# The moving operands of the projections are shifted by 16 bytes against the weights

## The chip, the cores and the metric

The kernel is one program on one core of a Trainium2 chip. The metric is the device time of one execution in microseconds (us): 2906.49 us is the median of three runs of the kernel before (2905.98 to 2910.71).

## The reference

Two blocks of two layers each work on x, 512 tokens by 1024 features in float32. Every layer has a mixer (mLSTM with neighbourhood attention, differential attention, HGRN2 with forgetting attention, RG-LRU with stick-breaking attention) and a gated feed-forward; the first block also has cross attention to 256 memory tokens. Each sublayer ends in a projection, a residual sum and a layer norm. What matters here are the products with the weight matrices:

```
proj = x @ w_in                       # mixers, q/k/v, memory
mix  = heads @ w_out
gate, up = split(x @ w_gu)            # 1024 -> 2 * 2816
ff   = (silu(gate) * up) @ w_down     # 2816 -> 1024
x    = layer_norm(alpha * x + mix or ff)
```

## The kernel before

x lies transposed, features on the 128 partitions, in eight tiles of 512 tokens. Every product is made of two float32r parts per operand: a high part (the rounded number) and a low part (the remainder). `mm3` (L271 to L276) issues three matmuls for each pair of 128 x 128 weights and 128 x 512 x: high with high (L274), weights high with x low (L275), weights low with x high (L276). In its call `matmul(out, a, b)` the first operand a is loaded into the array as weights (LDWEIGHTS, the stationary operand) and b streams past it (the moving operand). So each of the three has a weight load of its own, and TensorE alternates weight load, matmul, weight load, matmul. The program lists the matmuls' operands as moving,stationary: `p_mm<-xh,w_hi` is x's high part moving past the high part of the weights, into the PSUM tile `p_mm`.

`fetch` (L326) brings 128 x 1024 weights by DMA into `w_raw`, ScalarE rounds them into `w_hi` (L337), VectorE takes the remainder into `w_lo` (L339). `block_a` (L342) runs eight k-steps of `mm3` over one such block, 24 matmuls. `proj_a` (L349) does so for a list of blocks, either over all 512 tokens or, with `halves`, over 256 tokens at a time; `close_sublayer` (L411) always works on 256 tokens at a time. `proj_b` (L378) turns the roles round: parts of x (or of the memory) are the stationary operand and the weights move.

The operands of these products are: `XH` and `XL` (x's parts, tiles `xh`, `xl`, L219 and L220), the inner features of the feed-forward (`f_h`, `f_l`, L556 and L557), the parts of the memory (`mm_h`, `mm_l`, L603), keys, queries and values of the attentions, and `w_hi`, `w_lo`. A tile is a range of bytes in every partition of SBUF, laid down by the pools in the order of the program. No engine's order of work is touched here; the order is that of the code.

Where the tiles start, in bytes of a partition, modulo 256:

```
                      before                      after the change
w_hi, w_lo (all)      32                          32
xh, xl (x's parts)    32                          48
f_h, f_l              32                          48
mm_h, mm_l, m_kh      224                         224
x_qh, x_ql            32                          32
x_ph, x_pl            96                          96
m_v                   224                         224
dv / d_pt             128 / 0                     128 / 0
```

A slice of 128 or 256 float32 columns moves the start by a multiple of 256 bytes, so these remainders hold for every matmul on the tile.

Of the kernel before, what the change touches and what calls it, by code (L numbers as in the profile page):

```python
# [9 lines left out]
F32R = mybir.dt.float32r  # L10
# [6 lines left out]
P = 128  # L17
S = 512
D = 1024
KT = 8  # L20
# [33 lines left out]
def layout(i):  # L54
# [62 lines left out]
    for l in range(2):  # L117
        ffn(f"f{l}", f["ffn_w_gu"][l], f["ffn_w_down"][l])
        ffn(f"f{l + 2}", f["ffn_w13_2"][l], f["ffn_w2_2"][l])
# [87 lines left out]
class Prog:  # L207
    def __init__(self, ctx, tc, a):
        self.tc, self.nc, self.a = tc, tc.nc, a
        nc = tc.nc  # L210
        self.cp = ctx.enter_context(tc.tile_pool(name="cst", bufs=1))
        self.st = ctx.enter_context(tc.tile_pool(name="state", bufs=1))
        self.wp = ctx.enter_context(tc.tile_pool(name="wts", bufs=4))
        self.ps = ctx.enter_context(tc.tile_pool(name="ps", bufs=4, space=PSUM))
        st = self.st
        xf = st.tile([P, KT * S], F32, name="xf")
        self.XF = [xf[:, k * S : (k + 1) * S] for k in range(KT)]
        self.all_x = xf.rearrange("p (k s) -> p k s", k=KT)
        self.XH = [st.tile([P, S], F32R, name=f"xh{k}") for k in range(KT)]  # L219
        self.XL = [st.tile([P, S], F32R, name=f"xl{k}") for k in range(KT)]  # L220
        self.AO = [st.tile([P, S], F32, name=f"ao{k}") for k in range(KT)]
        cp = self.cp

        ones = cp.tile([P, 2 * P], F32, name="k_ones")
        nc.vector.memset(ones[:, 0:P], 1.0 / D)
        nc.vector.memset(ones[:, P : 2 * P], 1.0 / P)
        self.ones_d, self.ones_p = ones[:, 0:P], ones[:, P : 2 * P]
        nr = cp.tile([P, P], F32R, name="k_nr")
        nc.vector.tensor_scalar(nr, ones[:, P : 2 * P], -float(P), None, ALU.mult)
        self.mones_r = nr  # L230
        pr = cp.tile([P, P], F32R, name="k_pr")
        nc.vector.tensor_copy(pr, ones[:, P : 2 * P])
        self.ones_pr = pr
        cc = cp.tile([P, 4], F32, name="k_cc")
        nc.vector.memset(cc[:, 0:1], LN_EPS)
        nc.vector.memset(cc[:, 1:2], 1.0)
        self.eps, self.one = cc[:, 0:1], cc[:, 1:2]
        self.kv = {}
        self.pending = []
        self.biases = []  # L240
        self.before = []
        self.loaded = False
# [306 lines left out]
    def ffn(self, pre, ln, last=False):  # L549
        nc, tc, a = self.nc, self.tc, self.a  # L550
        with tc.tile_pool(name="ffn", bufs=2, reuse_waits="tile") as fp:
            off = 0
            for part, nt in enumerate(FPARTS):
                hs, ls = [], []
                for t in range(nt):
                    hs.append(fp.tile([P, S], F32R, name="f_h", tag="f_h", bufs=11))  # L556
                    ls.append(fp.tile([P, S], F32R, name="f_l", tag="f_l", bufs=11))  # L557

                def evac(n, ps, c0, c1, keep={}):
                    t = n // 2  # L560
                    c = slice(c0, c1)
                    if n % 2 == 0:
                        s = fp.tile([P, S], F32, name="f_s", tag="f_s", bufs=3)
                        nc.scalar.activation(s[:, c], ps[:, c], AF.Silu)
                        keep[t, c0] = s
                    else:
                        s = keep.pop((t, c0))
                        nc.vector.tensor_tensor(s[:, c], s[:, c], ps[:, c], ALU.mult)  # L568
                        self.tail = self.split(hs[t][:, c], ls[t][:, c], s[:, c])

                src = []
                for t in range(nt):
                    src += [a[pre + "_gu"][off + t], a[pre + "_gu"][FT + off + t]]
                if part == 0:
                    self.proj_a(src[:4], evac, halves=True)
                    self.proj_a(src[4:], lambda n, ps, c0, c1: evac(n + 4, ps, c0, c1), tags=("mm", "sc"))
                else:
                    self.proj_a(src, evac, tags=("mm", "sc"))
                off += nt
                d = a[f"{pre}_d{part}"]  # L580
                if part < len(FPARTS) - 1:
                    for m in range(8):
                        w = self.fetch(d[m], nt * P)
                        ps = self.mm(("mm", "sc")[m % 2])
                        self.block_a(w, ps, hs, ls)
                        self.add_partial(m, ps, part == 0)
                else:
                    self.close_sublayer([d[m] for m in range(8)], hs, ls, False, ln, last)
# [1013 lines left out]
```

## Time and profile before

| | us |
|---|---|
| median of three runs | 2906.49 |
| the profiled execution | 2910.26 |
| span of its instructions | 2908.3 |
| TensorE matmul busy | 2849.4 (98% of the span) |
| VectorE busy | 1694.3 (58%) |
| ScalarE busy | 1274.8 (44%) |
| mean granted TensorE clock | 0.996 of 2.4 GHz |

[...] What a stream costs is read from one start to the next. [...]

### The profile page before, as it was taken

Reading aid. Unit: us, or ns where it says so; the run is one execution under the profiler, and the core shown is the slowest. Engines: PE = TensorE matmul, PEld = TensorE weight load, DVE = VectorE, ACT = ScalarE, POOL = GpSimd, SP = SyncE. Lnnn points to the kernel's source line nnn. Section 1 sums busy time; section 2 is a strip of 40 time slices with the busy share of each in tenths; the row PEclk is TensorE's granted clock in tenths of the full one; section 3 lists DMA queues with packets and bytes.
Section 4 is the critical chain, followed back from the end, with each engine's and each line's share of the span. In section 5 each row is a group of like instructions: output and inputs, shape, how many; then the busy total and the mean of one; then the engine's idle time right before and its main releaser. Section 6 shows DMA issues by size and latency. Waiting matters only on the chain.

```text
span 2908.3 us, 40029 instructions
## 1 busy us (share of the span) xinstructions
PE 2849.4 (98%) x15354; PEld 2415.0 (83%) x15354; DVE 1694.3 (58%) x3164; ACT 1274.8 (44%) x2328; POOL 424.1 (15%) x500
## 2 busy tenths in 40 slices
PE   9999999999999999999999999999999999999998
PEld 7678989888886678898888988798888976988887
DVE  5877656333469887563333767873333759733335
ACT  4555544222256765442222644652222548532223
POOL 0402012000121121020000432230000302400003
PEclk9999999999999999999999999999999999999999
DMA  5232522333332225223332321223332331133232
GB/s 179 78 117 77 160 66 88 95 98 98 101 97 80 76 70 170 71 80 101 93 99 79 106 73 60 80 88 95 100 96 83 99 93 39 59 103 100 94 94 67
DMA packets 83071, 269.07 MB, mean 93 GB/s; under 512 B 10648, under 2 KB 15144, under 8 KB 82880
## 3 DMA queue, kind: packets, MB, share of 16 engines
q1 hardware_dynamic: 81376, 261.49, 29.3%
q0 software_dynamic: 1504, 5.04, 0.5%
q8 instruction: 120, 1.97, 0.3%
q14 instruction: 71, 0.58, 0.1%
HBM read 260.14 MB, written 2.15 MB: 90 GB/s over the span
## 4 chain that ended last, share of the span: by engine, by line
PE 78%; DVE 13%; ACT 4%; issue 3%; DMA 1%; POOL 0%; SPq 0%; DVEq 0%; ACTq 0%; POOLq 0%
PE p_mm L275 14%; PE p_mm L274 13%; PE p_mm L276 13%; PE p_sc L274 10%; PE p_sc L276 10%; PE p_sc L275 9%; DVE w_lo L339 2%; DVE ao L450 2%; PE p_tp L275 1%; PE p_tp L276 1%; PE p_tp L274 1%; DVE ac L742 1%; DVE xl L460 1%; PE p_sc L1264 1%; DVE ao L449 1%
## 5 line engine op out<-in xcount | busy, mean ns | idle before, releaser
L337 ACT ACTIVATE w_hi<-w_raw 128x1024 fp32r<-128x1024 f32 (+2 forms) x478 | 492.9, 1036 | 1108.6 <-PE p_mm L275 484.1
L339 DVE TENSOR_TENSOR w_lo<-w_raw,w_hi 128x512 fp32r<-128x512 f32 (+2 forms) x956 | 650.1, 710 | 501.9 <-ACT w_hi L337 495.6
L274 PE MATMUL p_mm<-xh,w_hi 128*128 128x512 f32 (+1 forms) x1920 | 688.8, 359 | 7.3 <-ACT w_hi L337 4.9
L275 PE MATMUL p_mm<-xl,w_hi 128*128 128x512 f32 (+1 forms) x1920 | 688.1, 358 | 5.6 <-DVE xl L460 3.6
L276 PE MATMUL p_mm<-xh,w_lo 128*128 128x512 f32 (+1 forms) x1920 | 683.5, 356 | 0.0
L275 PEld LDWEIGHTS p_mm<-xl,w_hi 128*128 128x128 f32 x1920 | 365.2, 190 | 59.0 <-DVE xl L460 6.5
L274 PEld LDWEIGHTS p_mm<-xh,w_hi 128*128 128x128 f32 x1920 | 365.0, 190 | 58.7 <-ACT w_hi L337 4.9
L276 PEld LDWEIGHTS p_mm<-xh,w_lo 128*128 128x128 f32 x1920 | 365.0, 190 | 49.5 <-issue 0.6
L276 PE MATMUL p_sc<-xh,w_lo 128*128 128x512 f32 (+1 forms) x1024 | 358.5, 350 | 0.9 <-DVE w_lo L339 0.9
L274 PE MATMUL p_sc<-xh,w_hi 128*128 128x512 f32 (+1 forms) x1024 | 359.3, 351 | 0.0
L275 PE MATMUL p_sc<-xl,w_hi 128*128 128x512 f32 (+1 forms) x1024 | 358.0, 350 | 0.0
L496 POOL TENSOR_TENSOR ao<-xf 128x256 f32<-128x256 f32 x20 | 19.9, 995 | 1695.6 <-DVE xf L489 1293.8
L568 DVE TENSOR_TENSOR f_s<-f_s,p_sc 128x512 f32<-128x512 f32 x80 | 55.1, 688 | 289.4 <-PE p_sc L276 289.4
L276 PEld LDWEIGHTS p_sc<-xh,w_lo 128*128 128x128 f32 x1024 | 193.7, 189 | 26.4 <-DVE w_lo L339 1.1
L274 PEld LDWEIGHTS p_sc<-xh,w_hi 128*128 128x128 f32 x1024 | 193.6, 189 | 25.8 <-issue 0.4
L275 PEld LDWEIGHTS p_sc<-xl,w_hi 128*128 128x128 f32 x1024 | 193.7, 189 | 25.3 <-issue 0.2
L274 PE MATMUL p_sc<-f_h,w_hi 128*128 128x512 f32 (+1 forms) x464 | 157.5, 339 | 0.0
L276 PE MATMUL p_sc<-f_h,w_lo 128*128 128x512 f32 (+1 forms) x464 | 157.2, 339 | 0.2
L275 PE MATMUL p_mm<-f_l,w_hi 128*128 128x512 f32 (+1 forms) x464 | 157.2, 339 | 0.0
L276 PE MATMUL p_mm<-f_h,w_lo 128*128 128x512 f32 (+1 forms) x464 | 156.7, 338 | 0.0
L274 PE MATMUL p_mm<-f_h,w_hi 128*128 128x512 f32 (+1 forms) x464 | 156.7, 338 | 0.0
L275 PE MATMUL p_sc<-f_l,w_hi 128*128 128x512 f32 (+1 forms) x464 | 156.7, 338 | 0.0
(438 smaller groups left out, 4699.2 us busy)
## 6 DMA issues: line engine op xcount, KB each, us to landing
w_raw<-in_f_gu SPq DMA_DIRECT2D x176, 512.0 KB, 3.5
w_raw<-in_w_e SPq DMA_DIRECT2D x70, 512.0 KB, 3.6
w_raw<-in_w_x SPq DMA_DIRECT2D x64, 512.0 KB, 3.9
w_raw<-in_w_o SPq DMA_DIRECT2D x64, 512.0 KB, 3.7
w_raw<-in_f_d SPq DMA_DIRECT2D x64, 448.0 KB, 3.2
w_raw<-in_f_d SPq DMA_DIRECT2D x32, 512.0 KB, 3.5
r_s<-r_t SPq DMA_DIRECT2D x64, 64.0 KB, 2.0
na_b<-in_na_bias SPq DMA_DIRECT2D x6, 384.0 KB, 3.0
```

The lines of the kernel that those rows point to most:

```text
L274: nc.tensor.matmul(out, wh, xh, start=start, stop=False)
L275: nc.tensor.matmul(out, wh, xl, start=False, stop=False)
L276: self.last = nc.tensor.matmul(out, wl, xh, start=False, stop=stop)
L337: nc.scalar.activation(hi[:, :n], raw[:, :n], AF.Copy)
L339: nc.vector.tensor_tensor(lo[:, c], raw[:, c], hi[:, c].bitcast(F32), ALU.subtract)
L449: eng.tensor_tensor(t, self.XF[m][:, c], mu, ALU.subtract)
L450: nc.vector.scalar_tensor_tensor(t, t, g, r, ALU.mult, ALU.mult)
L460: nc.vector.scalar_tensor_tensor(xl, t, b, xh.bitcast(F32), ALU.add, ALU.subtract)
L496: eng.tensor_tensor(sm, self.XF[order[0]][:, c], self.XF[m][:, c], ALU.add)
L568: nc.vector.tensor_tensor(s[:, c], s[:, c], ps[:, c], ALU.mult)
L742: nc.vector.scalar_tensor_tensor(out, xp[:, j : j + S], w[j], out, ALU.mult, ALU.add)
L1264: nc.tensor.matmul(ps[:, c * 64 : c * 64 + 64].rearrange("p (n h) -> p n h", h=hl), x[:, cs], halves(x[:, cs], hl)[1], start=True, stop=True,)
```

## The change

All parts of x become slices of one tile `xs` that is 64 elements longer than its sixteen parts and skips its first 4 elements (16 bytes). Every tile of the inner features is made 64 elements (256 bytes) longer, and its first 4 elements are skipped. The weights' tiles start where they did, modulo 256. The engines issue the same instructions in the same order as before, with other addresses; one wait of ScalarE and four of the DMA queue name another matmul, since tiles that share room with them lie elsewhere.

```
-        self.XH = [st.tile([P, S], F32R, name=f"xh{k}") for k in range(KT)]
-        self.XL = [st.tile([P, S], F32R, name=f"xl{k}") for k in range(KT)]
+
+        xs = st.tile([P, 2 * KT * S + 64], F32R, name="xs")
+        xs = [xs[:, 4 + k * S : 4 + (k + 1) * S] for k in range(2 * KT)]
+        self.XH, self.XL = xs[:KT], xs[KT:]
...
-                    hs.append(fp.tile([P, S], F32R, name="f_h", tag="f_h", bufs=11))
-                    ls.append(fp.tile([P, S], F32R, name="f_l", tag="f_l", bufs=11))
+                    hs.append(fp.tile([P, S + 64], F32R, name="f_h", tag="f_h", bufs=11)[:, 4 : S + 4])
+                    ls.append(fp.tile([P, S + 64], F32R, name="f_l", tag="f_l", bufs=11)[:, 4 : S + 4])
```

## Rows read from the trace of the kernel before

**Rows 1.** The page: busy time of each engine, and the granted clock in 40 slices.

```profile
PE 2849.4 (98%) x15354; PEld 2415.0 (83%) x15354; DVE 1694.3 (58%) x3164; ACT 1274.8 (44%) x2328; POOL 424.1 (15%) x500
PEclk9999999999999999999999999999999999999999
```

**Rows 2.** TensorE's waits, longest in total first: us, times, longest.

```profile
PE p_mm L274 <- ACT w_hi L337: 4.9, 1, 4.9
PE p_sc L435 <- DVE ao L499: 4.4, 3, 1.8
PE p_mm L275 <- DVE xl L460: 3.6, 7, 0.9
```

**Rows 3.** Matmul groups by form: line, names, shape, count, busy us, mean ns.

```profile
L275 PE MATMUL p_mm<-xl,w_hi 128*128 128x512 f32 x1280 | 502.0, 392 | 0.0
L275 PE MATMUL p_sc<-xl,w_hi 128*128 128x512 f32 x640 | 249.0, 389 | 0.0
L275 PE MATMUL p_mm<-xl,w_hi 128*128 128x256 f32 x640 | 186.1, 291 | 5.6 <-DVE xl L460 3.6 <-POOL xl L463 1.7
L275 PE MATMUL p_sc<-xl,w_hi 128*128 128x256 f32 x384 | 109.0, 284 | 0.0
L275 PE MATMUL p_mm<-f_l,w_hi 128*128 128x512 f32 x240 | 93.4, 389 | 0.0
L275 PE MATMUL p_mm<-f_l,w_hi 128*128 128x256 f32 x224 | 63.8, 285 | 0.0
L275 PE MATMUL p_tp<-xl,w_hi 128*128 128x256 f32 x192 | 54.3, 283 | 0.0
L275 PE MATMUL p_mm<-w_lo,xh 128*128 128x512 f32 x96 | 37.4, 389 | 0.0
L276 PE MATMUL p_sc<-x_ph,m_v 128*128 128x512 f32 x32 | 12.6, 393 | 0.0
```

**Rows 4.** Timeline of TensorE, feed-forward, 512 tokens: start us, record's us.

```profile
1499.78 0.39 PE L274 MATMUL p_mm<-f_h,w_hi 128*128 128x512 f32 x1
...
1512.47 0.39 PE L276 MATMUL p_sc<-f_h,w_lo 128*128 128x512 f32 x1
```

**Rows 5.** The same, close of a feed-forward, 256 tokens.

```profile
799.80 0.28 PE L275 MATMUL p_sc<-f_l,w_hi 128*128 128x256 f32 x1
...
801.48 0.28 PE L274 MATMUL p_mm<-f_h,w_hi 128*128 128x256 f32 x1
```

**Rows 6.** The same, keys of the memory, 256 tokens.

```profile
309.77 0.28 PE L274 MATMUL p_mm<-mm_h,w_hi 128*128 128x256 f32 x1
...
312.61 0.28 PE L275 MATMUL p_sc<-mm_l,w_hi 128*128 128x256 f32 x1
```

**Rows 7.** Weight loads by form, in the stretch 800 to 812 us.

```profile
L274 PEld LDWEIGHTS p_mm<-f_h,w_hi 128*128 128x128 f32 x17 | 3.3, 192 | 0.0
```

**Rows 8.** Weight loads by form, in the stretch 306 to 312.9 us.

```profile
L274 PEld LDWEIGHTS p_mm<-mm_h,w_hi 128*128 128x128 f32 x8 | 1.5, 188 | 0.0
```

**Rows 9.** Weight loads by form, in the stretch 1500 to 1600 us.

```profile
L274 PEld LDWEIGHTS p_mm<-xh,w_hi 128*128 128x128 f32 x56 | 10.5, 188 | 2.2
```

**Rows 10.** Timeline of TensorE, values of the memory: weights move, memory parts stationary.

```profile
317.18 0.39 PE L275 MATMUL p_mm<-w_lo,mm_h 128*128 128x512 f32 x1
...
320.84 0.39 PE L276 MATMUL p_mm<-w_hi,mm_l 128*128 128x512 f32 x1
```

**Rows 11.** Timeline and group of the float32 values product in differential attention.

```profile
934.59 3.59 PE L1152 MATMUL p_tp<-d_pt,dv 128*128 128x512 f32 x8
L1152 PE MATMUL p_tp<-d_pt,dv 128*128 128x512 f32 x56 | 25.4, 596 | 0.4 <-DVE d_pt L1147 0.3
```

**Rows 12.** Stretches: busy us (and instructions) of PE, PEld, DVE, ACT, POOL; clock, DMA.

```profile
491.00:790.00 299.00, 298.96 (x1357) 249.01 (x1356) 109.12 (x172) 80.44 (x99) 3.19 (x4) 1.00 0.30 94
790.10:813.30 23.20, 23.20 (x193) 23.10 (x192) 17.51 (x34) 11.39 (x23) 11.26 (x13) 1.00 0.37 112
814.00:831.80 17.80, 17.80 (x109) 15.76 (x108) 16.34 (x37) 11.49 (x25) 8.99 (x11) 1.00 0.34 105
```

**Rows 13.** ScalarE groups of 128 x 512 that write from PSUM.

```profile
L816 ACT ACTIVATE xp<-p_mm 128x512 f32<-128x512 f32 x8 | 4.6, 580 | 0.0
L264 ACT ACTIVATE x_qh<-p_mm 128x512 fp32r<-128x512 f32 x16 | 9.3, 581 | 0.0
```

## The prediction

> **What bounds the kernel now.** I read the page first. TensorE is busy for 2849.4 of 2908.3 us and its clock stands at full speed in all 40 slices [rows 1], so 2.4 GHz is the rate to compare with. Then its waits: the longest in total is 4.9 us, once [rows 2], so no other engine holds it up for long. What is left is how fast matmuls follow each other, which the busy share does not tell. For that I took the timeline of TensorE and divided from one start to another by the number of starts between. In the feed-forward, over 512 tokens, there are 56 steps from 1499.78 to 1512.47 us, 226.6 ns each [rows 4]. 512 columns at one per clock are 213.3 ns, so each matmul with its weight load loses 13.3 ns. Over 256 tokens there are 14 steps from 799.80 to 801.48 us, 120.0 ns each [rows 5], against 106.7: again 13.3 ns. So the loss belongs to the pair of matmul and weight load, and not to the columns.
>
> **A second placement is in the trace already.** The keys of the memory are made with the same weights, moving operands of 256 columns and the same three matmuls, but the memory's parts start at 224 modulo 256 where the weights start at 32: the moving operand lies 64 bytes ahead of the weights. There 25 steps from 309.77 to 312.61 us take 113.6 ns each [rows 6]. That is 6.4 ns less than with both at 32. The weight load agrees: its record is 192 ns in the slow stretch [rows 7] and 188 ns in this one [rows 8]. In the stream of 512 columns it is 188 ns with both operands at 32 [rows 9], so there the weight load shows no delay although the matmul loses 13.3 ns.
>
> Another placement has the parts of the memory as stationary operand at 224 and the weights moving at 32, 64 bytes behind: 16 steps from 317.18 to 320.84 us, 228.8 ns each [rows 10], 2.2 ns more than with both at the same remainder. And a float32 matmul, which goes at half the column rate, takes (3.59 - 0.596) / 7 = 0.428 us a pass over 512 columns [rows 11], 1.0 ns over the 426.7 of its columns, with a weight load for each pass as well. So the loss is not that of a weight load as such. It is there when the moving operand is read at full rate, and how large it is depends on where the two operands lie.
>
> **What the change touches.** It moves the operands of 12,816 matmuls. Moving x parts or inner features over 512 tokens: (1280 + 640) x 3 of x, 240 x 6 of the inner features and 48 into the transposes' banks, 7248 together; over 256 tokens: (640 + 384 + 192) x 3 and 224 x 6, 4992 together; stationary x parts: 96 x 6 = 576 [rows 3], where L275 stands for L274 and L276 of the same form. For the first two the moving operand comes to lie 16 bytes behind the weights, for the last 16 bytes ahead. No row has a distance of 16 bytes: those that the trace shows are multiples of 32.
>
> **The price per matmul, from both sides.** At 256 columns: the best that a row gives for the same weights is 113.6 ns, 6.4 less. The floor is 1.0 ns over the columns, as in the float32 pass: 12.3 ns less. On the other side the rows with the moving operand behind the weights cost 2.2 ns more at 64 bytes [rows 10], and at 128 bytes (`x_ph` at 96, `m_v` at 224) a record of 393 ns instead of 389 [rows 3], 4 ns more. I take 6.4 ns off at 256 columns: there the weight load itself is late when both lie at the same remainder, and in the one other placement with the same operands that is gone. At 512 columns I take nothing: the weight load is not late there, and the nearest row, both at 32, is the present one. For the 576 I take nothing for the same reason.
>
> Sum: 4992 x 6.4 ns = 31.9 us. Is it on the path that sets the end? In the close of a feed-forward the second half of the tokens has VectorE at 16.34 of 17.80 us and TensorE at 17.80 [rows 12]. Its 109 instructions would give back 0.7 us, to 17.1, still above VectorE's 16.34, which works meanwhile. In the first half VectorE has 17.51 of 23.20 us. So TensorE stays the later one; if VectorE's work could not overlap as well as that, a tenth of the gain would stay behind. The weights come fast enough: the DMA share in these stretches is 0.34 to 0.37 [rows 12].
>
> The other engines write and read the shifted tiles too. I cost that at nothing. ScalarE writes `xp` 8 bytes behind the start of its tile and takes 580 ns, against 581 for `x_qh`, which starts at its tile's start [rows 13]. A longer write would lie beside TensorE's work in any case, except at the layer norms, where each of the 160 or so pieces could cost some ns. The longer tiles take 256 bytes each and displace no buffer. The five waits that name another matmul are on ScalarE and on the queue of the weights' DMA, which have idle time there (80.44 us busy of 299.00 on ScalarE [rows 12]).
>
> The profiled execution took 2910.26 us, 3.8 above the median of 2906.49. From its time the sum gives 2878.4, from the median 2874.6. I say **2875 us**, and for this case alone 2862 to 2895.
>
> **Rivals.**
>
> *The 512-column matmuls gain too.* Both widths lose the same 13.3 ns [rows 4, 5], which speaks for one cause; a cause that one shift removes at 256 columns it may well remove at 512. With 6.4 ns each, 12,240 x 6.4 = 78.3 us, 2828 us. At the floor of the float32 pass it is 12,240 x 12.3 = 150.6 us, 2756 us. Against it: the 188 ns of [rows 9], and that at 512 columns no placement in the trace goes faster than 226.6. [...]
>
> *Nothing happens.* The two reads do not meet at all, and the 6.4 ns come from another difference between the stages, such as what VectorE and ScalarE read meanwhile. Or 16 bytes are too little to part what 64 bytes part. Then it stays at 2906 us. For it: the nearest placement to 16 bytes is the present one. Against it: the record of the weight load goes with the placement [rows 7, 8], and both stages have VectorE and ScalarE at work. [...]
>
> *Slower: the loss grows with the distance behind the weights.* Ahead by 64 bytes 6.9 ns are lost, level 13.3, behind by 64 bytes 15.4 [rows 5, 6, 10]. That is monotone, and the shift goes the wrong way. If a stalled stream has to slide until it is clear of the other, 16 bytes more mean 16 x 6.4 / 64 = 1.6 ns by the steep part, or 16 x 2.2 / 64 = 0.5 ns by the flat part. On 12,240 matmuls that is 19.6 or 6.7 us: 2926 or 2913 us, and I take 2920. It decides as soon as the loss at 16 bytes exceeds 13.3 ns in the feed-forward. Against it: a loss that repeats every 256 bytes has to fall back somewhere, and right behind level, where one stream passes the other, is the likely place.
>
> **How the numbers follow.** Forecast 0.42, the 512-column gain 0.22, nothing 0.15, slower 0.21. What a measurement of this kernel tells from no change is 0.2%, 5.8 us. The first two cases are below that bound but for 0.01, the slower one is above it but for 0.01: faster 0.63, same 0.17, slower 0.20. The range holds the forecast, the middle of the second case and most of the slower one: 2800 to 2926. Left out are the deep end of the second case, some 0.09, and a loss as large as that of 128 bytes behind (4 ns on 7248, 29 us), some 0.06.
>
> **What would show it.** In the profile after, 24 matmuls of a close over 256 tokens take 24 x 113.6 ns = 2.73 us instead of 2.88, with weight loads of 188 ns; the feed-forward over 512 tokens keeps its 226.6 ns; the memory's keys keep 113.6. The second case shows as steps of 220 ns or less in the feed-forward. The slower one shows as 227 to 228 ns there. The forecast is wrong if the 256-column step stays at 120 ns, or if most of the time comes from the 512-column stretches, which hold (7248 + 576) x 226.6 ns = 1773 us and so 55 us per 7 ns.

## The result, and the profile after

After the change the median is 2934.17 us (six runs, 2930.24 to 2936.4); the kernel before, beside it on the same chip, 2908.28 us. The ratio is 1.0086, with a 95% interval from 1.0073 to 1.0099: slower by 25.9 us, where 2875 us had been forecast. The lines of `mm3` are 276, 277 and 278 now.

The page of the changed kernel, answering to [rows 1]: TensorE is busy for the same share, 98%, at a granted clock of 0.997 (0.996 before), for 26.0 us more.

```profile
PE 2875.4 (98%) x15354; PEld 2407.6 (82%) x15354; DVE 1691.3 (58%) x3164; ACT 1274.7 (43%) x2328; POOL 424.0 (14%) x500
PEclk9999999999999999999999999999999999999999
```

Its waits, longest in total first (us, times, longest), answering to [rows 2]: no new wait has come.

```profile
PE p_sc L437 <- DVE ao L501: 5.3, 5, 1.7
PE p_mm L276 <- ACT w_hi L339: 4.9, 1, 4.9
```

So the matmuls themselves follow each other more slowly. The next two groups of matmuls answer to the `p_mm<-f_l,w_hi` rows of [rows 3] (389 and 285 ns): a record over 512 tokens is 5 ns longer, one over 256 tokens 4 ns shorter.

```profile
L277 PE MATMUL p_mm<-f_l,w_hi 128*128 128x512 f32 x240 | 94.6, 394 | 0.0
L277 PE MATMUL p_mm<-f_l,w_hi 128*128 128x256 f32 x224 | 62.8, 281 | 0.2
```

To read the stream itself, a window is cut exactly from the first start of a stage to the first start of what follows; its length over the number of matmuls is the step, the time from one start to the next. The length of a record is no step: over 512 tokens it is 389 ns [rows 3], and the next matmul starts after 226.6 ns [rows 4]. (The count in the row is one to three higher, since records at the edges overlap it.) The windows of the first feed-forward of the kernel before: the whole 512-token part (1320 matmuls), the first stage in it that reads the inner features (192), and the two parts of its close (189 and 147 matmuls over 256 tokens). The columns are the window, its length, the busy time and count of PE, PEld, DVE, ACT, POOL, the granted clock and the DMA.

```profile
480.50:779.72 299.22, 299.22 (x1322) 247.83 (x1321) 105.56 (x164) 77.36 (x94) 0.00 (x0) 1.00 0.31 95
545.80:589.32 43.52, 43.52 (x193) 36.05 (x192) 16.46 (x25) 9.04 (x9) 0.00 (x0) 1.00 0.32 97
779.72:802.92 23.20, 23.16 (x191) 22.78 (x189) 15.41 (x26) 10.09 (x16) 10.56 (x12) 1.00 0.47 148
803.60:821.42 17.82, 17.82 (x150) 17.79 (x149) 16.92 (x34) 12.25 (x29) 8.42 (x10) 1.00 0.10 30
```

The same stretches of the changed kernel:

```profile
480.14:785.93 305.79, 305.79 (x1322) 248.19 (x1321) 105.59 (x164) 77.46 (x94) 0.00 (x0) 1.00 0.30 93
546.85:591.33 44.48, 44.48 (x193) 36.10 (x192) 16.46 (x25) 9.04 (x9) 0.00 (x0) 1.00 0.31 95
785.93:808.91 22.98, 22.92 (x190) 22.51 (x189) 15.31 (x26) 10.10 (x16) 10.48 (x12) 1.00 0.47 150
809.59:826.94 17.35, 17.35 (x150) 17.32 (x148) 16.82 (x34) 11.99 (x28) 8.32 (x9) 1.00 0.10 31
```

The 512-token part takes 6.57 us more (44.48 / 192 = 231.7 ns a step against 226.7), the close 0.22 + 0.47 us less. Four feed-forwards have such parts. Over all steps of the execution, from start to start, those of 512 columns sum to 31.5 us more and those of 256 columns to 7.3 us less; with 0.6 us less for the float32 products of these widths that makes 23.6, and the span grew by 23.4 us. The memory's keys, which the change does not move, are 1.0 us longer; more on them below. The other engines do not take part. The groups of ScalarE and VectorE that write the shifted inner features, in the same stretch, take 633 and 685 ns (632 and 686 before):

```profile
L266 ACT ACTIVATE f_h<-f_s 128x512 fp32r<-128x512 f32 x20 | 12.7, 633 | 5.4 <-DVE f_s L570 5.4
L268 DVE TENSOR_TENSOR f_l<-f_s,f_h 128x512 fp32r<-128x512 f32 x20 | 13.7, 685 | 0.8 <-ACT f_h L266 0.7
```

And the weight loads in the second part of the close (809.6 to 826.9 us) have come down from the 192 ns of [rows 7] to 188, as forecast, though the step of the closes came down from 119.9 to 116.8 ns only:

```profile
L276 PEld LDWEIGHTS p_mm<-f_h,w_hi 128*128 128x128 f32 x21 | 3.9, 188 | 0.0
```

Over 512 tokens (546.85 to 591.33 us) the load is at 188 ns as in [rows 9], although the step has grown by 5 ns:

```profile
L277 PEld LDWEIGHTS p_mm<-f_l,w_hi 128*128 128x128 f32 x32 | 6.0, 188 | 1.4
```

### The profile page after: what moved, and what is told of

Read it like the earlier page. It is cut to its first block, busy times and chain, and to the rows that moved or that the text cites. A ratio compares the mean times of both kernels' runs of the same rounds, so it can differ in the third digit from the quotient of the medians.

```text
span 2931.7 us, 40029 instructions
## 1 busy us (share of the span) xinstructions
PE 2875.4 (98%) x15354; PEld 2407.6 (82%) x15354; DVE 1691.3 (58%) x3164; ACT 1274.7 (43%) x2328; POOL 424.0 (14%) x500
## 4 chain that ended last, share of the span: by engine, by line
PE 75%; DVE 12%; ACT 3%; issue 2%; DMA 1%; POOL 1%; SPq 0%; DVEq 0%; ACTq 0%; POOLq 0%
PE p_mm L277 13%; PE p_mm L276 13%; PE p_mm L278 13%; PE p_sc L276 9%; PE p_sc L278 9%; PE p_sc L277 9%; DVE w_lo L341 2%; DVE ao L452 2%; PE p_tp L278 1%; PE p_tp L277 1%; PE p_tp L276 1%; DVE xs L462 1%; DVE ao L451 1%; PE p_sc L326 1%; PE p_sc L1266 1%
## 5 line engine op out<-in xcount | busy, mean ns | idle before, releaser
L276 PE MATMUL p_mm<-xs,w_hi 128*128 128x512 f32 (+1 forms) x1920 | 691.2, 360 | 7.2 <-ACT w_hi L339 4.9
L277 PE MATMUL p_mm<-xs,w_hi 128*128 128x512 f32 (+1 forms) x1920 | 691.4, 360 | 6.6 <-DVE xs L462 4.1
L278 PE MATMUL p_mm<-xs,w_lo 128*128 128x512 f32 (+1 forms) x1920 | 686.5, 358 | 0.0
L277 PEld LDWEIGHTS p_mm<-xs,w_hi 128*128 128x128 f32 x1920 | 362.4, 189 | 66.0 <-DVE xs L462 7.2
L276 PEld LDWEIGHTS p_mm<-xs,w_hi 128*128 128x128 f32 x1920 | 362.4, 189 | 63.1 <-ACT w_hi L339 4.9
L278 PEld LDWEIGHTS p_mm<-xs,w_lo 128*128 128x128 f32 x1920 | 362.4, 189 | 54.3 <-issue 0.6
L278 PE MATMUL p_sc<-xs,w_lo 128*128 128x512 f32 (+1 forms) x1024 | 360.7, 352 | 1.0 <-DVE w_lo L341 1.0
L276 PE MATMUL p_sc<-xs,w_hi 128*128 128x512 f32 (+1 forms) x1024 | 361.5, 353 | 0.0
L277 PE MATMUL p_sc<-xs,w_hi 128*128 128x512 f32 (+1 forms) x1024 | 360.2, 352 | 0.0
L278 PEld LDWEIGHTS p_sc<-xs,w_lo 128*128 128x128 f32 x1024 | 192.4, 188 | 29.4 <-DVE w_lo L341 1.2
L276 PEld LDWEIGHTS p_sc<-xs,w_hi 128*128 128x128 f32 x1024 | 192.4, 188 | 28.8 <-issue 0.4
L277 PEld LDWEIGHTS p_sc<-xs,w_hi 128*128 128x128 f32 x1024 | 192.4, 188 | 28.5 <-issue 0.2
```

The lines of the kernel that those rows point to most:

```text
L276: nc.tensor.matmul(out, wh, xh, start=start, stop=False)
L277: nc.tensor.matmul(out, wh, xl, start=False, stop=False)
L278: self.last = nc.tensor.matmul(out, wl, xh, start=False, stop=stop)
```

## The experiments

"Behind" is how many bytes the moving operand begins behind the weights, modulo 256; "ahead" is the other way; "level" is the same remainder. Steps are means from start to start over steps without a wait. Where no ratio is given, the kernel was run once.

**The weights shifted too.** Everything at 48: level again.

```
-        hi = pool.tile([P, 1024], F32R, name="w_hi", tag="w_hi", bufs=4)
-        lo = pool.tile([P, 1024], F32R, name="w_lo", tag="w_lo", bufs=4)
+        hi = pool.tile([P, 1024 + 64], F32R, name="w_hi", tag="w_hi", bufs=4)[:, 4:1028]
+        lo = pool.tile([P, 1024 + 64], F32R, name="w_lo", tag="w_lo", bufs=4)[:, 4:1028]
```

> The changed kernel, with the weights' tiles (w_hi, w_lo) moved by 16 bytes as well, so that x, the inner features and the weights all start at 48 modulo 256: level again, but none at a multiple of 32. Theory A, the distance between moving operand and weights sets the step: the steps of before return, 226.6 ns at 512 columns and 120 ns at 256, time about 2908 us. Theory B, a moving operand that starts 16 bytes off a multiple of 32 is read more slowly, whatever the weights do: 231.7 ns at 512 columns, time about 2934 us.

Measured: 2934.66 us, ratio 1.0097 [1.0080, 1.0113]. Windows of TensorE, the 192-matmul stage of three feed-forwards:

```profile
546.48:590.64 44.16, 44.16 (x194) 1.00 0.32 95
2032.05:2076.85 44.80, 44.80 (x193) 1.00 0.32 94
2635.84:2680.22 44.38, 44.38 (x194) 1.00 0.33 95
```

That is 230.0, 233.3 and 231.1 ns. Level is not enough: theory A, distance alone, fell. Theory B has the whole time about right but not the step, which is not even the same for the same placement in one program.

**The inner features at other distances, multiples of 32.** The kernel before, with the features 192, 128, 64 and 32 bytes behind in the four feed-forwards; x stays level at 32.

```
+            at = {'f0': 192, 'f1': 128, 'f2': 64, 'f3': 32}[pre] // 4
-                    hs.append(fp.tile([P, S], F32R, name="f_h", tag="f_h", bufs=11))
+                    hs.append(fp.tile([P, S + 64], F32R, name="f_h", tag="f_h", bufs=11)[:, at : S + at])
...
```

> The kernel before, with x as it was and the inner features shifted by 192, 128, 64 and 32 bytes against the weights in the four feed-forwards in turn. Only the down projections (f_h, f_l moving) are read: over 512 tokens and, in the close, over 256. Theory A (distance): 192 bytes gives 113.6 ns at 256 columns as the keys of the memory had; 64 bytes gives 228.8 ns at 512 columns and 128 bytes 231 to 233 ns; 32 bytes lies between level (226.6) and 64 or is as slow as 16 (231.7). Theory B (alignment to 32 bytes): all four are multiples of 32 and give 226.6 and 120 ns. Whole time within 10 us of 2908 by either.

Measured: 2916.53 us. Windows of TensorE: the 192-matmul stage of the four feed-forwards, with an x stage of 336 matmuls behind the first; then the second part of the close of the first and the third.

```profile
546.03:590.83 44.80, 44.80 (x194) 1.00 0.31 95
590.83:667.01 76.18, 76.18 (x338) 1.00 0.31 92
1361.01:1405.81 44.80, 44.80 (x194) 1.00 0.32 95
2026.87:2070.83 43.96, 43.96 (x194) 1.00 0.33 96
2623.44:2668.25 44.81, 44.81 (x194) 1.00 0.32 94
805.19:822.05 16.86, 16.86 (x149) 1.00 0.10 32
2284.50:2302.00 17.50, 17.50 (x150) 1.00 0.11 31
```

233.3, 233.3, 229.0 and 233.4 ns, while x, level in the same feed-forward, keeps 76.18 / 336 = 226.7. So multiples of 32 are not free either, and theory B fell as well. The close gains: 17.82 us became 16.86 at 192 behind (64 ahead, the distance of the memory's keys; 113.7 ns a step) and 17.50 at 64 behind.

**The shift alone, and distances ahead.** The same edit with 16, 240, 224 and 160 bytes behind (the last three are 16, 32 and 96 ahead).

```
+            at = {'f0': 16, 'f1': 240, 'f2': 224, 'f3': 160}[pre] // 4
```

> As the run with 192, 128, 64 and 32 bytes, now with 16, 240, 224 and 160 bytes in the four feed-forwards. Theory A (distance): 16 gives 231.7 and 117 to 118 ns as in the changed kernel although x is level again; 240, 224 and 160 go their own way, 240 near 232 ns at 512 columns, as the weights moving past x's parts did in the changed kernel. Theory B (alignment): 16 and 240 give 231.7 ns, 224 and 160 give 226.6 and 120 ns. The sawtooth that I had in mind in the prediction would show as a step well under 226.6 ns at one of the placements right before or behind level.

Measured: 2913.98 us. Windows of TensorE as in the experiment before:

```profile
544.01:588.49 44.48, 44.48 (x194) 1.00 0.32 95
588.49:664.68 76.19, 76.19 (x338) 1.00 0.31 92
1358.20:1403.00 44.80, 44.80 (x193) 1.00 0.32 94
2023.56:2068.37 44.81, 44.81 (x194) 1.00 0.32 94
2620.63:2665.60 44.97, 44.97 (x193) 1.00 0.32 94
```

The first two rows are the change cut down to one operand: features shifted by 16 bytes take 231.7 ns a step, as in the changed kernel to the hundredth of a microsecond for the stage, and x, not shifted, takes 226.8 in the stage behind it. On the other side of level it is 233.3, 233.4 and 234.2 ns. The loss does not fall back on either side.

**The longer tiles without the shift.** All the padding of the change and of the shifted weights, with every operand at its old remainder.

```
+        xs = [xs[:, k * S : (k + 1) * S] for k in range(2 * KT)]
+        hi = pool.tile([P, 1024 + 64], F32R, name="w_hi", tag="w_hi", bufs=4)[:, 0:1024]
+                    hs.append(fp.tile([P, S + 64], F32R, name="f_h", tag="f_h", bufs=11)[:, 0:S])
...
```

> The layout of the run with the weights shifted too (x in one tile, inner features and weights with 256 bytes of padding), but every operand at its tile's start: all at 32 modulo 256, as before. It tells whether the padding, which moves tiles against each other by multiples of 256 bytes, costs anything. Theory C, the start modulo 256 of each operand sets the step and the padding costs nothing: 226.7 ns at 512 columns, 120 ns at 256, time 2908 us. Theory D, the pitch of the tiles (distances modulo 512 or more) is what slowed the two kernels: 230 to 233 ns, time about 2930 us.

Measured: 2907.89 us, ratio 0.9998 [0.9989, 1.0008]; the steps are 226.7 and 119.9 ns as before. Other room and other pitches, with every start as it was, cost nothing here. This kernel showed something else, in stages that no experiment aimed at. The memory's keys are made twice, and their operands are 64 bytes ahead in this kernel, in the one before and in the changed one alike. Windows of 96 of their matmuls in each of the two stages, first the kernel before:

```profile
294.61:305.69 11.08, 11.08 (x98) 1.00 0.81 240
1106.90:1118.00 11.10, 11.10 (x99) 1.00 0.72 216
```

the changed kernel:

```profile
293.38:304.87 11.49, 11.49 (x98) 1.00 0.76 230
1112.16:1123.24 11.08, 11.08 (x98) 1.00 0.74 219
```

and this one:

```profile
293.68:304.76 11.08, 11.08 (x99) 1.00 0.84 237
1104.96:1116.46 11.50, 11.50 (x99) 1.00 0.70 222
```

Each window holds one wait of 0.3 us. Without it the steps are 113.3 ns in the short ones and 117.8 in the long ones, nearly throughout a stage. One placement thus has two states, and the kernel before happened to have both stages in the better one.

The same is seen at 512 columns. The changed kernel has five stages in which parts of x are the stationary operand and the weights move, 16 bytes ahead of them. Four take some 233 ns a step (232.7 to 233.4), and one takes 226.9, as much as level. Here are 86 matmuls of that one, and 86 of one of the four:

```profile
1697.37:1716.86 19.49, 19.49 (x87) 1.00 0.33 92
2374.75:2394.82 20.07, 20.07 (x88) 1.00 0.00 1
```

These stages read the same tiles of x and of the weights, so the addresses alone do not decide which step a stage gets.

**All at 0, and 64 behind and ahead of it.** Weights and x at 0, the features at 0, 0, 64 and 192.

```
+        xs = [xs[:, 56 + k * S : 56 + (k + 1) * S] for k in range(2 * KT)]
+        hi = pool.tile([P, 1024 + 64], F32R, name="w_hi", tag="w_hi", bufs=4)[:, 56:1080]
+            at = {"f0": 56, "f1": 56, "f2": 8, "f3": 40}[pre]
...
```

> As the run with padding alone, with the weights and x at 0 modulo 256, and the inner features at 0, 0, 64 and 192 in the four feed-forwards. Level at 32 is the fastest placement at 512 columns so far (226.7 ns), level at 48 was 230 to 233. If what counts is being level and on a multiple of 32, level at 0 gives 226.7 ns again, 64 behind 229.0 and 64 ahead 233.3 ns at 512 and 113.7 at 256, as with the weights at 32. If the absolute start counts as well, these shift; a start on a multiple of 64 could then be better than 32, with 220 ns as 33 slots of 6.67 ns.

Measured: 2912.02 us. The 192-matmul stage of the first, third and fourth feed-forward:

```profile
548.03:591.55 43.52, 43.52 (x194) 1.00 0.33 97
2023.24:2067.21 43.97, 43.97 (x193) 1.00 0.32 95
2620.26:2665.06 44.80, 44.80 (x193) 1.00 0.31 95
```

226.7 ns level, 229.0 at 64 behind and 233.3 at 64 ahead: the same numbers as with the weights at 32 (226.7, 229.0 and 233.3). Between 32 and 0, at these three distances, only the distance counts at 512 columns. No stage came to the 220 ns of the expectation.

**Level at 16.** Weights and x at 16, the features at 16, 16, 0 and 32.

```
+        xs = [xs[:, 60 + k * S : 60 + (k + 1) * S] for k in range(2 * KT)]
+        hi = pool.tile([P, 1024 + 64], F32R, name="w_hi", tag="w_hi", bufs=4)[:, 60:1084]
+            at = {"f0": 60, "f1": 60, "f2": 56, "f3": 0}[pre]
...
```

> Weights and x at 16 modulo 256, the inner features at 16, 16, 0 and 32 in the four feed-forwards (level, level, 16 bytes ahead, 16 behind). Levels at 0 and 32 gave 226.7 ns at 512 columns, level at 48 gave 230 to 233. If a start that is no multiple of 32 costs even when level, level at 16 gives 230 to 233 ns and the whole kernel about 2930 us. If 48 was special (or the level run was slow for another reason), level at 16 gives 226.7. With the moving operand on a multiple of 32 and the weights not, the third and fourth feed-forward tell whose start counts: 226.7 if only the moving operand's, 230 or more if the weights' or the distance.

Measured: 2933.84 us. The 192-matmul stage of the first, second and fourth feed-forward:

```profile
547.81:592.61 44.80, 44.80 (x194) 1.00 0.32 94
1368.22:1412.38 44.16, 44.16 (x194) 1.00 0.33 96
2638.78:2682.63 43.85, 43.85 (x194) 1.00 0.32 96
```

Level at 16 gives 233.3 in one and 230.0 in the other; 16 behind it, 228.4. With 48 above, two level placements off the multiples of 32 are slow, and with 0 and 32 (and 224 below) three on them are not.

**Only the low weights moved.** The kernel before with `w_lo` 64 bytes on, at 96: the moving operand is level with the weights of two matmuls of three, and 64 ahead of those of the third.

```
-        lo = pool.tile([P, 1024], F32R, name="w_lo", tag="w_lo", bufs=4)
+        lo = pool.tile([P, 1024 + 64], F32R, name="w_lo", tag="w_lo", bufs=4)[:, 16:1040]
```

> The kernel before, with the low parts of the weights alone 64 bytes further. Per k-step the three matmuls are high weights with high x, high weights with low x, low weights with high x. If what counts is the distance between a moving operand and the weights loaded meanwhile for the next matmul, the second matmul's step changes (its next weights lie 64 bytes behind it); if it is the distance to the matmul's own weights, the third one's. At 512 columns a lone step 64 bytes ahead should take more than 226.7 ns (233.3 where all were 64 ahead), at 256 columns less than 120. If the steps are locked to each other, all three change together, and the run can't tell.

Measured: 2930.24 us. The 192-matmul stage of the first feed-forward, and then the weight loads in the second part of its close:

```profile
546.87:591.25 44.38, 44.38 (x194) 1.00 0.32 95
```

```profile
L276 PEld LDWEIGHTS p_mm<-f_h,w_lo 128*128 128x128 f32 x21 | 4.0, 192 | 0.0
L275 PEld LDWEIGHTS p_mm<-f_l,w_hi 128*128 128x128 f32 x21 | 4.0, 188 | 0.0
L274 PEld LDWEIGHTS p_mm<-f_h,w_hi 128*128 128x128 f32 x21 | 3.9, 188 | 0.0
```

The mean of 231.1 ns is 228.3 after the start of the first matmul of a triple, 229.2 after the second and 235.8 after the third, which has the moved weights. So the distance to a matmul's own weights seems to weigh most at 512 columns, not that to the weights loaded meanwhile. But all three changed from 226.7. In the close the load of the moved weights stays at 192 ns while the other two, level as before, come down to 188; the same pattern, though, stands in a close of the next experiment (800.99 to 818.49 us), where both parts of the weights are moved alike, so it does not point to the moved weights:

```profile
L276 PEld LDWEIGHTS p_mm<-f_h,w_lo 128*128 128x128 f32 x21 | 4.0, 192 | 0.0
```

What makes all three slower stays open.

**The weights moved for the 256-token work alone.** In the closes and in `proj_a` over halves the weights start at 96, so that x and the features lie 64 ahead; at 512 columns all stays level.

```
+    def fetch(self, src, n=1024, pool=None, at=0):
+        hi = pool.tile([P, 1024 + 64], F32R, name="w_hi", tag="w_hi", bufs=4)[:, at : at + 1024]
+        ws = [self.fetch(s, at=16) for s in src]
...
```

> The kernel before, with the weights of all matmuls of 256 moving columns (closes of the sublayers, first blocks of a stage) 64 bytes further: weights at 96, x and inner features at 32 as before, so that the moving operand lies 64 bytes ahead, as the memory's parts do. The 512-column matmuls stay level. If the distance modulo 256 sets the step at 256 columns, 113.7 ns instead of 120 on some 4950 matmuls: 31 us less, 2877 us. If the absolute starts count (moving at 224 and weights at 32 was what gave 113.7), the step lies between 115 and 118 ns: 10 to 20 us less, about 2893 us. If padding costs (theory D), no gain.

Measured: 2898.78 us, ratio 0.9966 [0.9954, 0.9979]. Windows of TensorE in the first feed-forward, the 192-matmul stage and the second part of the close:

```profile
543.56:587.08 43.52, 43.52 (x194) 1.00 0.33 97
800.99:818.49 17.50, 17.50 (x150) 1.00 0.11 31
```

The 512-column step stays at 226.7, and faster than before it is. But this close is at 117.8 ns a step, not 113.7.

**The features moved in the closes, the weights for x.** The features of the closes go to 224 and their weights stay at 32; for x over halves the weights go to 96.

```
+                at = 48 if part == 2 else 0
+                    hs.append(fp.tile([P, S + 64], F32R, name="f_h", tag="f_h", bufs=11)[:, at : S + at])
+                    w = self.fetch(src[m], n * P, more_w if m > 3 else None, at=16 if first else 0)
...
```

> The run with the weights of the 256-column matmuls moved, but in the close of the feed-forwards with the weights at 32 and the inner features at 224 (64 ahead in this way gave 113.7 ns in two runs; with the weights at 96 the same close took 115.6 to 117.8). If the absolute place counts, 113.7 ns on these 1344 matmuls: 4 us below the run with the weights moved, about 2895 us. If the two states, 113.5 and 118 ns, come at random at one distance, the time stays within 3 us of 2899.

Measured: 2896.49 us, ratio 0.9963 [0.9949, 0.9977]. The second part of the close in the first and second feed-forward:

```profile
799.77:816.63 16.86, 16.86 (x149) 1.00 0.11 32
1609.75:1626.62 16.87, 16.87 (x150) 1.00 0.15 46
```

All four closes of the feed-forward are at 113.7 ns, as if the absolute place counted; the next run speaks against that. x over halves is at 116.1 in the mean, a mixture of both states.

**Everything at 224, weights at 32 where 256 tokens are worked on.** Level at 224 for 512 columns, 64 ahead for 256.

```
+        xs = [xs[:, 48 + k * S : 48 + (k + 1) * S] for k in range(2 * KT)]
+    def fetch(self, src, n=1024, pool=None, at=48):
+        ws = [self.fetch(s, at=0) for s in src]
+                    hs.append(fp.tile([P, S + 64], F32R, name="f_h", tag="f_h", bufs=11)[:, 48 : S + 48])
...
```

> x and all inner features at 224 modulo 256; the weights at 224 too for matmuls of 512 columns, and at 32 for those of 256 columns (closes, first blocks, the memory's keys). So the wide ones are level on a multiple of 32 and the narrow ones have the moving operand 64 bytes ahead, in the one placement (224 before 32) that held 113.7 ns throughout. If that placement does it: 4992 x 6.2 ns = 31 us less than before, about 2877 us. If the two states of the narrow stream, 113.7 and 117.8 ns, depend on how a stretch is entered, x's closes stay near 116 ns and the time near 2890 us. If level at 224 is not as good as at 0 and 32, the wide ones lose 3 ns or more and it is slower than before by 20 us.

Measured: 2893.71 us, ratio 0.9950 [0.9937, 0.9964], the lowest of all and faster than both kernels; the two experiments before it have intervals that overlap with this one. Windows of TensorE: the 192-matmul stage of the first feed-forward, the second part of the close of the first and of the second:

```profile
542.06:585.58 43.52, 43.52 (x194) 1.00 0.33 97
798.77:815.64 16.87, 16.87 (x150) 1.00 0.11 32
1607.60:1625.10 17.50, 17.50 (x149) 1.00 0.14 44
```

512 columns at 224 are as good as at 32. At 256 columns three closes of the feed-forward are in the state of 113.7 ns and one in that of 117.8. All four read the same tiles, so the place, absolute or relative, does not choose between the two. Over the whole execution the steps without a wait give back 19.7 us on x and 6.9 on the features, and the steps on x that do wait take 10.7 us more (216 such steps instead of 190), which leaves 15.9 of the 26.6 us; the medians differ by 14.1.

All placements together (ns per step; where an experiment had several stages, the lowest and highest):

| moving operand against the weights | 512 columns | 256 columns |
|---|---|---|
| level, at 0, 32 or 224 | 226.7 | 119.9 (at 0 and 32) |
| level, at 16 or 48 | 230.0 to 233.3 | 116.7 to 118.3 |
| 16 behind | 228.4 to 231.7 | 115.0 to 118.7 |
| 32 behind | 233.2 to 233.4 | 117.3 |
| 48 behind (values of the memory, weights at 16) | 233.3 | not tried |
| 64 behind | 228.9 to 229.5, in two stages 233.1 and 233.2 | 115.6 to 117.8 |
| 80 behind (values of the memory, weights at 48) | 231.1 to 231.2 | not tried |
| 128 behind | 233.3 | 118.7 |
| 96 ahead | 234.2 | 117.4 |
| 80 ahead (memory's keys, weights at 48) | not tried | 118.7 to 118.8 |
| 64 ahead | 233.3 | 113.3, 117.8 or a mixture |
| 48 ahead (memory's keys, weights at 16) | not tried | 122.6 to 123.1 |
| 32 ahead | 233.4 | 118.3 |
| 16 ahead | 232.7 to 233.4, in one stage 226.9 | 117.2 to 118.3 |

## Why the prediction was wrong

**The step that failed** is "At 512 columns I take nothing: the weight load is not late there, and the nearest row, both at 32, is the present one". It measured 5.0 ns more on the features (226.7 to 231.7), 4.6 on x and, in the mean, 4.9 where parts of x are the stationary operand. On 1440, 5680 and 562 steps without a wait that is 7.2 + 26.1 + 2.8 = 36.1 us. The steps of these operands that wait took 2.9 us back, and the other products of 512 columns, which the change does not move, came out 1.7 us shorter: 31.5 us in all. The change's own shift does it, on one operand alone as well (231.7 ns for the shifted features, 226.8 for x beside them). The reading behind the step was wrong: a weight load record of 188 ns [rows 9] was taken to mean that the placement did not matter at 512 columns. It does not tell that: in the changed kernel the load is at 188 ns too, with a step of 231.7. The placement was the best one there already, and only a loss was left to get. The two rows of other placements at 512 columns, 2.2 and 4 ns more [rows 3, 10], both spoke for a loss; the sum priced it at nothing, and the 4 ns, 29 us, were left out of the range with a chance of 0.06. That is about what came.

**The 256-column gain** had the right sign and a quarter of its size: 7.3 us of 31.9. The 6.4 ns came from one stage [rows 6], in another placement (64 ahead) and, as the memory's keys showed later, in the better one of two states. At 16 behind the features gave 3.2 ns and x 1.6. The sign that the memory's keys keep their 113.6 ns failed in one of their two stages, at 117.8, though the change does not move them. That the weight load would come down to 188 ns was right, but it does not fix the step: at 188 ns steps of 113.7, 116.8 and 117.8 were all seen (the last at 64 behind, with the weights at 0).

**What held.** TensorE's matmul rate is the bound, at a granted clock of 0.997, and no wait replaced the time (the longest in total is 5.3 us). The column times of 213.3 and 106.7 ns are borne out by a difference: no page gives the clock in GHz, but the 256 columns more of [rows 4] take 226.6 - 120.0 = 106.6 ns [rows 4, 5], 2.40 columns a ns. That the float32 matmuls go at half this rate stands in the trace of the kernel before: `p_sc<-g,av` takes 429 ns from start to start over 512 columns and 216 over 256 (92.69 to 96.89 us), 213 ns for 256 columns more. The other engines' writes to the shifted tiles cost nothing (633 and 685 ns against 632 and 686), the longer tiles neither (0.9998). VectorE stayed shorter than TensorE in the close. The rows read for that were cut some 10 us late: [rows 12] called 790.1 to 831.8 us the close, but it runs from 779.72 to 821.42 us. In its second part VectorE has 16.92 us of 17.82, nearer to the bound than the 16.34 of the text; the gain there still reached the end, 17.35 us.

**The rivals.** *Slower* came true, at 2934 us instead of 2920, but not by its mechanism: the loss does not grow with the distance (233.4 ns at 32 behind, 229.0 at 64, 233.3 at 128). Its monotone row took 64 ahead from 256 columns and 64 behind from 512; at 512 columns the features 64 ahead lose 20.0 ns, not 6.9. What was held against it, that the loss "has to fall back somewhere, and right behind level ... is the likely place", fell: 16 behind gave 228.4 to 231.7 ns, and ahead of all the weights the features took 233.3 to 234.2; only the one stage of x's parts above kept 226.9. *The 512-column gain* fell: no placement went below 226.7 ns. *Nothing happens* fell, at both widths: the same matmuls with the same loads take 226.7 or 233.3 ns over 512 columns, and 113.7 or 119.9 over 256, by where the operands begin.

**What stays open.** Why a common remainder of 16 or 48 is not as good as 0, 32 or 224, and what decides between the two states of one placement, which the addresses do not. Each kernel has one profile, so whether a state changes from one execution to the next is not shown. That the start of the operands is the cause of the loss is shown, by the shift of one operand alone and by the padding without a shift; by which mechanism is not: no trace shows single reads, so reads that meet, or a stream that stalls and slides, are the author's picture and not a measurement.

## What to carry to other kernels

In this kernel, where weight load and matmul alternate, the start of the operands was worth up to 3% of the step at 512 columns (226.7 to 234.2 ns) and 5% at 256 (113.7 to 119.9): take the step from start to start for every placement that the trace already holds, for each width by itself and in more than one stage, since one placement had two steps here (113.3 and 117.8 ns), and don't carry a gain from one width to the other. Here moving operands of 512 columns were fastest level with the weights at 0, 32 or 224 (226.7 ns), and those of 256 columns were slow there (119.9 ns at 0 and 32) and fastest, in one of its two steps, 64 ahead (113.3; 117.8 in the other). So in this kernel the weights' start had to follow the width of the work, which gave a ratio of 0.9950. And when the only rows for other placements show a loss, they are the estimate, not the edge of it.

## What the runs showed of the hardware

- The mean steps seem to lie on a grid. 113.3, 120.0, 226.7 and 233.3 ns are 17, 18, 34 and 35 times 6.67 ns, which is what 16 columns take by [rows 4, 5] (106.6 ns for 256). In the close of the changed kernel single steps alternate between 114 and 119 or 120 ns. Means between, as 230.0, 231.1 and 231.7, fit a half, two thirds and three quarters of the way from 34 to 35. Other means, as 229.0 and 234.2, do not fit; single steps of 512 columns, at 227 to 235 ns in a repeating pattern, do not keep to the grid one by one.
- Level on a multiple of 32 (0, 32 and 224 were tried) was the best placement tried at 512 columns: it gave 226.7 or 226.8 ns in every feed-forward stage. Every other placement gave 228.4 or more, except in one stage of the changed kernel, 226.9 at 16 ahead. At 256 columns the same, at 0 and 32, was nearly the worst (119.9): only 48 ahead of weights at 16 was slower (122.6 to 123.1).
- One placement held two steps, each for a whole stage: 113.3 and 117.8 ns at 64 ahead, 230.0 and 233.3 level at 16, 226.9 and 233.4 at 16 ahead, each pair in one program and with the same tiles.
- At 64 ahead over 256 columns the weight loads tell the two apart: in the memory's keys all are at 188 ns where the step is 113.3 (kernel before, both stages) and one in three is at 192 where it is 117.8 (changed kernel, 293.38 to 304.87 us); level at 32, in the second part of the first close of the kernel before, all are at 192 (119.9).
